# Expert weights: each load waits for the load three places ahead of it, in place of two

## The chip, the cores and the metric

One core of a Trainium2 chip runs the whole program as one launch. The metric is the device time of a run in microseconds (us); of the kernel before, three runs stand below, and one further execution was recorded by the hardware profiler. All rows in this document come from that one recorded execution unless something else is said.

## The reference, cut to what matters

Two transformer blocks run one after the other on 512 tokens of 1024 features in float32. The first block (dilated attention, a gated recurrence, an MLP) and the first half of the second (gated linear attention, a state-space layer) end in a router, and what follows it is a mixture of experts with 32 experts, of which each token takes 4:

```python
def moe_ffn(h, router_w, router_b, w_gu, b_gu, w_down, b_down):
    logits = (xt @ router_w + router_b).astype(f32)
    top_val, top_idx = lax.top_k(logits, TOP_K)          # 4 of 32
    gate = jax.nn.softmax(top_val, axis=-1)
    ...
    def expert_block(args):
        xblk, e = args
        gu = xblk @ w_gu[e] + b_gu[e]                    # 1024 -> 2048
        g, up = gu[:, :D_FF_2], gu[:, D_FF_2:]
        g = jnp.minimum(g, SWIGLU_LIMIT)
        up = jnp.clip(up, -SWIGLU_LIMIT, SWIGLU_LIMIT)
        act = (up + 1.0) * (g * jax.nn.sigmoid(SWIGLU_ALPHA * g))
        return act @ w_down[e] + b_down[e]               # 1024 -> 1024
    ...
    out = zeros.at[tok_buf].add(yb * w_buf[:, None])
```

The weights of one expert are 8 MB for `w_gu` and 4 MB for `w_down`; all 32 experts together are 384 MB, read once from HBM.

## The kernel before

The blocks ahead of the experts take roughly the first 980 us. They aren't touched. Everything around the change is in the class `Moe` (from line 1329).

**Weights.** `order` (L1760) fixes the sequence of the loads: the eight `gu` loads of expert 0, then for each expert e the eight `gu` loads of expert e+1 and the four `dn` loads of expert e. That is 32 x 12 = 384 loads of 1 MB each. `load` (L1625) takes the next of them, gives it the next of 21 slots in SBUF in turn (`RING = 5, 16`), and issues it on SyncE's queue: L1635 for a `gu` load (tile `wgu`, 128 rows of 8 KB) and L1638 for a `dn` load (tile `wdn`). A load into a slot waits until TensorE has read the slot's former weights for the last time. Besides that, `turn` (L1642) makes each load wait for the landing of an earlier one:

```python
        if limit and len(self.flight) >= FLIGHT:
            self.g.tc.add_manual_dep(d, self.flight[-FLIGHT], ... DependencyClass.Sync ..., reason="few loads at a time")
        self.flight.append(d.name)
```

`flight` lists all loads in the order of issue, so with `FLIGHT = 2` at most two are under way. The first five loads are issued before the router is through, with `limit` False, that is without this wait; the other 16 of the first round follow when their slots exist (`buffers`, L1507). SyncE works in order: a load that waits holds back all loads behind it. In the stage of the experts SyncE issues nothing else, apart from reading the experts' token counts and following the branches. `finish` (L1836) sends five small loads through `turn` as well, at the very end.

**Experts.** `run` (L1800) goes through the experts: `tile_up(e)` multiplies the tokens of expert e with the `gu` weights, `tile_down(e-1)` those of the expert before with the `dn` weights, and the loads for the slots that come free are issued behind each (eight, then four). The first 64 tokens of an expert are always computed (L1587 for `gu`, L1617 for `dn`): eight matmuls, two column halves in turn, for each load. Further matmuls run only when the expert has more than 64, 96 or 128 tokens (L1591, and again L1587 and L1617 with the tile `turned`), behind branches on the counts; the expert's weights stay in their slots until these are through. GpSimd gathers the tokens (L1531, `xg`, `x`, `late`), adds the results into HBM (L1623, `acc`), and moves activations of large experts out and in (`spill`, `late`), all on its own DMA queue. TensorE transposes tokens and activations (L1539, `ptx`), VectorE and ScalarE compute the activation (L1560 to L1564) and ScalarE scales the result (L1621).

Of the kernel before, what the change touches and what calls it, by code (L numbers as in the profile page):

```python
# [1316 lines left out]
NCH = T // CH  # L1317
QUARTERS = 2
RING = 5, 16
FLIGHT = 2  # L1320
LATE = 9
PACE = 2
FILLS = 8
# [3 lines left out]
class Moe:  # L1327
# [314 lines left out]
    def turn(self, d, limit=True):  # L1642

        if limit and len(self.flight) >= FLIGHT:
            self.g.tc.add_manual_dep(d, self.flight[-FLIGHT], mybir.DependencyInfo(mybir.DependencyClass.Sync, mybir.DependencyReason.SCHED_ONLY), reason="few loads at a time")
        self.flight.append(d.name)
# [301 lines left out]
```

## Time and profile before

| | us |
|---|---|
| median of 3 runs | 2337.91 |
| lowest, highest | 2332.89, 2342.59 |
| the profiled execution | 2348.3 |
| its span, first to last instruction | 2346.5 |
| TensorE busy in it | 2046.9 |
| stage of the experts, first matmul with expert weights to the last | about 984 to 2310 |

PE is TensorE's matmuls, PEld its weight loads, DVE VectorE, ACT ScalarE, POOL GpSimd, SP SyncE; a q behind an engine's name is its sequencer. The profiled execution was 10.4 us longer than the median of the runs (0.4%). The 16 DMA engines are shown together: their share is the time that packets took, summed over the 16 and divided by 16 times the stretch. The granted clock of TensorE is given as a share of its upper level, 2.4 GHz; 0.961 is the mean of the span.

### The profile page before, as it was taken

How to read it: one execution, taken by the hardware profiler on the slowest of the kernel's cores; microseconds unless marked ns; L12 is line 12 of the kernel's file. 1: busy time of each engine (PE TensorE's matmuls, PEld its weight loads, DVE VectorE, ACT ScalarE, POOL GpSimd, SP SyncE). 2: the span in 40 equal slices, each digit the busy share in tenths (PEclk: the TensorE clock that was granted, in tenths of full speed). 3: DMA queues.
4: the chain of work that ended last, by engine and by line, in shares of the span. 5: the costliest groups of instructions: out<-in, count | busy, mean ns of one | idle time of the engine just before them, and what ended most of it. 6: DMA issues, size and time to landing. Idle time of an engine off the chain costs nothing. (4 is left out here: it accounts for less than half of the span.)

```text
span 2346.5 us, 31249 instructions
## 1 busy us (share of the span) xinstructions
PE 2046.9 (87%) x11586; PEld 1116.4 (48%) x11589; DVE 860.5 (37%) x1891; ACT 476.4 (20%) x839; POOL 333.1 (14%) x329
## 2 busy tenths in 40 slices
PE   6999988999998999789898997766798899898763
PEld 6856765688877977533333332221233333333211
DVE  6466659764556556522121121111121122121112
ACT  3345332234434124200100100000000110000001
POOL 2000226310013221100101101000001110101002
PEclk9999999999999999789999999999999999999997
DMA  6451476852237625898939899999996799999986
GB/s 194 119 169 52 154 195 187 252 175 92 98 104 213 213 75 196 345 337 292 327 143 323 300 337 331 356 329 337 325 356 231 257 329 330 336 349 342 333 323 204
DMA packets 213970, 584.24 MB, mean 249 GB/s; under 512 B 32287, under 2 KB 107438, under 8 KB 179822
## 3 DMA queue, kind: packets, MB, share of 16 engines
q1 hardware_dynamic: 182688, 523.74, 62.3%
q0 software_dynamic: 16784, 46.94, 7.4%
q10 hardware_dynamic: 14142, 9.10, 1.3%
q8 instruction: 189, 3.10, 0.5%
q14 instruction: 167, 1.37, 0.2%
HBM read 537.88 MB, written 41.84 MB: 247 GB/s over the span
## 5 line engine op out<-in xcount | busy, mean ns | idle before, releaser
L1587 PE MATMUL pg<-wgu,xT 128*64 128x512 f32 x1024 | 281.5, 620 | 77.9 <-DMA wgu<-in_exp_w_gu 72.5
L1587 PE MATMUL pu<-wgu,xT 128*64 128x512 f32 x1024 | 272.5, 603 | 3.5 <-issue 3.5
L1617 PE MATMUL py<-wdn,aT 128*64 128x512 f32 x1024 | 241.7, 604 | 34.0 <-DMA wdn<-in_exp_w_down 33.9
L1547 DVE TENSOR_TENSOR turned<-ptx,cols 128x512 f32<-128x512 f32 x42 | 29.1, 692 | 461.7 <-PE ptx L1539 460.4
L1561 ACT ACTIVATE th<-gm 128x512 f32<-128x512 f32 (+1 forms) x54 | 30.2, 560 | 777.4 <-DVE gm L1560 762.9
L89 DVE TENSOR_TENSOR wlo<-wst,whi 128x1024 fp32r<-128x1024 f32 (+1 forms) x109 | 135.4, 1242 | 126.6 <-ACT whi L88 126.5
L88 ACT CAST whi<-wst 128x1024 fp32r<-128x1024 f32 (+2 forms) x121 | 123.9, 1027 | 257.7 <-DMA wst<-in_w_ff_in 82.5
L1587 PEld LDWEIGHTS pg<-wgu,xT 128*64 128x64 f32 x1024 | 66.7, 139 | 228.5 <-DMA wgu<-in_exp_w_gu 124.5
L1587 PEld LDWEIGHTS pu<-wgu,xT 128*64 128x64 f32 x1024 | 76.6, 140 | 155.1 <-issue 155.1
L1623 POOL DMA_INDIRECT acc<-y,idx x54 | 85.7, 1587 | 445.5 <-ACTq L1745 226.0
L1617 PEld LDWEIGHTS py<-wdn,aT 128*64 128x64 f32 x1024 | 66.2, 136 | 166.4 <-issue 105.8
L1657 DVE CAST sel<-pick 128x128 fp32r<-128x128 f32 x32 | 7.7, 239 | 357.5 <-PEq L1735 151.1
L1591 PE MATMUL pgu<-wgu,turned 128*32 128x512 f32 x1152 | 128.6, 594 | 0.0
L98 PE MATMUL pf<-hTh,whi 128*128 128x512 f32 (+1 forms) x288 | 111.2, 390 | 8.6 <-ACT whi L88 6.2
L100 PE MATMUL pf<-hTh,wlo 128*128 128x512 f32 (+1 forms) x288 | 109.5, 383 | 6.9 <-DVE wlo L89 6.9
L99 PE MATMUL pf<-hTl,whi 128*128 128x512 f32 (+1 forms) x288 | 109.5, 381 | 0.0
L1531 POOL DMA_INDIRECT xg<-hn,idx x32 | 33.1, 1033 | 491.8 <-PE ptx L1539 415.5
L1617 PE MATMUL py<-wdn,turned 128*32 128x256 f32 (+1 forms) x1280 | 101.2, 418 | 0.0
L98 PE MATMUL plt<-whi,ahi 128*128 128x512 f32 x256 | 99.6, 389 | 0.0
L99 PE MATMUL plt<-wlo,ahi 128*128 128x512 f32 x256 | 99.6, 389 | 0.0
L100 PE MATMUL plt<-whi,alo 128*128 128x512 f32 x256 | 99.1, 389 | 0.0
L1560 DVE TENSOR_SCALAR gm<-pg 128x512 f32<-128x512 f32 x36 | 24.9, 691 | 155.0 <-PE pg L1587 150.4
(541 smaller groups left out, 3423.8 us busy)
## 6 DMA issues: line engine op xcount, KB each, us to landing
wgu<-in_exp_w_gu SPq DMA_DIRECT2D x256, 1024.0 KB
wdn<-in_exp_w_down SPq DMA_DIRECT2D x128, 1024.0 KB
wst<-in_w_in SPq DMA_DIRECT2D x36, 512.0 KB
wst<-in_w_ff_in SPq DMA_DIRECT2D x32, 512.0 KB
wst<-in_w_ff_out SPq DMA_DIRECT2D x32, 512.0 KB
ada_w<-in_ada_w SPq DMA_DIRECT2D x24, 512.0 KB
a<-in_ada_w SPq DMA_DIRECT2D x24, 512.0 KB
wst<-in_w_out SPq DMA_DIRECT2D x16, 512.0 KB
```

The lines of the kernel that those rows point to most:

```text
L88: g.nc.scalar.copy(hi, st)
L89: eng.tensor_tensor(out=lo, in0=st, in1=hi.bitcast(F32), op=ALU.subtract)
L98: g.nc.tensor.matmul(out, ah, bh, start=start, stop=False)
L99: g.nc.tensor.matmul(out, ah, bl, start=False, stop=False)
L100: g.nc.tensor.matmul(out, al, bh, start=False, stop=stop)
L1531: self.g.nc.gpsimd.indirect_dma_start(out=x, out_offset=None, in_=self.hn, in_offset=bass.IndirectOffsetOnAxis(ap=self.idx[2][:, c, e:e + ...
L1547: g.nc.vector.tensor_tensor(out=out, in0=src, in1=col(1), op=ALU.mult)
L1561: nc.scalar.activation(th, gm, AF.Tanh, scale=0.851)
L1587: nc.tensor.matmul(ps[h * w:(h + 1) * w, :], lhs, W[k][:, o + h * N:o + (h + 1) * N], start=False, stop=(k == KD - 1))
L1591: nc.tensor.matmul(both[h * w:(h + 1) * w], lhs, wk[:, h], start=False, stop=(k == KD - 1))
L1617: nc.tensor.matmul(py[h * w:(h + 1) * w, :], lhs, W[k // 2][:, o:o + N], start=False, stop=(k == KD - 1))
L1623: nc.gpsimd.indirect_dma_start(out=acc, out_offset=bass.IndirectOffsetOnAxis(ap=self.idx[n][:, c, e:e + 1], axis=0), in_=y, in_offset=None ...
```

## The change

```diff
--- before.py
+++ after.py
@@ -1317,7 +1317,7 @@
 NCH = T // CH
 QUARTERS = 2
 RING = 5, 16
-FLIGHT = 2
+FLIGHT = 3
 LATE = 9
 PACE = 2
 FILLS = 8
```

`FLIGHT` is read in `turn` alone. A load that went through `turn` with `limit` now waits for the landing of the load three places ahead of it in `flight`, and no longer for that two places ahead. The order of the loads, the slots, the waits for slots and all other instructions are written as before.

## Rows read from the trace of the kernel before

**Rows 1.** The page, 40 slices of 58.7 us: TensorE's busy tenths, GB/s of all DMAs
```profile
PE   6999988999998999789898997766798899898763
GB/s 194 119 169 52 154 195 187 252 175 92 98 104 213 213 75 196 345 337 292 327 143 323 300 337 331 356 329 337 325 356 231 257 329 330 336 349 342 333 323 204
```

**Rows 2.** Busy time by stretch: stretch, length, five engines (instructions), TensorE clock, DMA share, GB/s
```profile
984.00:1323.00 339.00, 310.37 (x1858) 111.84 (x1858) 63.23 (x113) 26.77 (x47) 38.95 (x32) 0.95 0.80 288
1410.00:1686.00 276.00, 192.49 (x892) 59.79 (x896) 40.51 (x69) 18.07 (x29) 22.69 (x18) 0.98 0.93 336
1880.00:2157.00 277.00, 261.88 (x1658) 96.38 (x1654) 56.56 (x104) 26.02 (x45) 33.57 (x25) 0.99 0.94 340
2157.00:2278.00 121.00, 83.19 (x351) 24.41 (x351) 17.60 (x30) 7.54 (x12) 7.81 (x6) 0.97 0.92 331
```

**Rows 3.** TensorE's waits from 1410 to 1686: who, for what, us, times, longest
```profile
PE pg L1587 <- DMA wgu<-in_exp_w_gu: 46.5, 35, 4.7
PE py L1617 <- DMA wdn<-in_exp_w_down: 24.5, 20, 2.3
```

**Rows 4.** TensorE's waits from 2157 to 2278
```profile
PE pg L1587 <- DMA wgu<-in_exp_w_gu: 26.0, 22, 3.7
PE py L1617 <- DMA wdn<-in_exp_w_down: 9.5, 8, 1.9
```

**Rows 5.** Timeline of TensorE: start, us, what, count [idle before it and what ended it]
```profile
1567.62 1.94 PE L1617 MATMUL py<-wdn,aT 128*64 128x512 f32 x8 [1.36 <-DMA wdn<-in_exp_w_down]
...
2298.91 7.09 PE L1617 MATMUL py<-wdn,aT 128*64 128x512 f32 x32
```

**Rows 6.** SyncE's waits from 1323 to 1686: who, for what, us, times, longest
```profile
SPq L1635 <- DMA wgu<-in_exp_w_gu: 154.9, 54, 6.2
SPq L1638 <- DMA wdn<-in_exp_w_down: 53.8, 17, 5.3
SPq L1635 <- DMA wdn<-in_exp_w_down: 50.6, 18, 3.9
SPq L1638 <- DMA wgu<-in_exp_w_gu: 49.2, 18, 4.4
SPq L1638 <- PEq L1713: 5.0, 1, 5.0
```

**Rows 7.** Load issues from 1323 to 1686, by line: count, ns min/median/max, first and last start
```profile
L1635 SPq DMA_DIRECT2D wgu<-in_exp_w_gu x72: 327/328/341, 1332.9 to 1674.3; - x72
...
L1638 SPq DMA_DIRECT2D wdn<-in_exp_w_down x37: 367/378/920, 1323.1 to 1680.4; - x37
```

**Rows 8.** Load issues from 1880 to 2278, by line
```profile
L1635 SPq DMA_DIRECT2D wgu<-in_exp_w_gu x80: 327/328/341, 1890.0 to 2270.3; - x80
...
L1638 SPq DMA_DIRECT2D wdn<-in_exp_w_down x41: 367/378/422, 1880.3 to 2277.4; - x41
```

**Rows 9.** Load issues of L1635 from 945 to 951, then from 914 to 918
```profile
L1635 SPq DMA_DIRECT2D wgu<-in_exp_w_gu x3: 328/328/383, 945.7 to 950.4; - x3
...
L1635 SPq DMA_DIRECT2D wgu<-in_exp_w_gu x5: 328/422/685, 914.5 to 917.6; - x5
```

**Rows 10.** Busy time from 921 to 929, columns as in rows 2
```profile
921.00:929.00 8.00, 8.00 (x49) 6.38 (x49) 3.82 (x11) 2.27 (x7) 0.00 (x0) 1.00 0.99 415
```

**Rows 11.** DMA queues from 1410 to 1686: packets, MB, share of 16 engines
```profile
q1 hardware_dynamic: 15458, 87.24, 85.4%
q0 software_dynamic: 2032, 4.85, 6.8%
q8 instruction: 27, 0.44, 0.6%
```

**Rows 12.** All DMA issues, GpSimd's indirect ones: count, median us from issue to landing
```profile
acc<-y,idx POOLq DMA_INDIRECT x54, 7.6
xg<-hn,idx POOLq DMA_INDIRECT x32, 6.3
```

**Rows 13.** TensorE's waits from 1686 to 2157, the longest alone
```profile
PE ptx L1539 <- DMA late<-spill: 7.5, 1, 7.5
```

## The prediction

> **What bounds the kernel now.** I read the slices of the page first. TensorE is busy for 9 tenths or so of most slices, but there are two dips, around slices 24 to 27 and at the end, and in both the DMAs move 323 to 356 GB/s [rows 1]. So I cut the stage of the experts into stretches. In those from 984 to 1323 and from 1880 to 2157 TensorE is busy for 310 of 339 and 262 of 277 us; from 1410 to 1686 (A) it is busy for 192.5 of 276 and from 2157 to 2278 (B) for 83.2 of 121 [rows 2]. The view of TensorE's waits names what is missing in A and B: weights. In A it waits 46.5 + 24.5 = 71.0 us in 55 pieces for loads [rows 3], in B 26.0 + 9.5 = 35.5 us in 30 pieces [rows 4]; from 984 to 1323 and from 1686 to 2157 that view has no such line.
>
> These rows are a little short. Eight matmuls on one load are shown as 1.94 us when they stand alone, but 32 in a row as 7.09 [rows 5]: the other 24 took 7.09 - 1.94 = 5.15 us, or 1.72 for each eight, so the last matmul's modelled end hides 0.22 us of each wait. With it A has 71.0 + 55 x 0.22 = 83 us and B 35.5 + 30 x 0.22 = 42 us of real waiting. Their sum, 125 us, is what endless bandwidth could give and no more.
>
> Then the queue of the loads. From 1323 to 1686 SyncE waits 154.9 + 53.8 + 50.6 + 49.2 = 308.5 us for landings, in 107 pieces, and 5 us for a slot [rows 6], while it issues 72 + 37 = 109 loads between 1323.1 and 1680.4 [rows 7]: 357.3 / 108 = 3.31 us a load. From 1880 to 2278 it is 121 loads from 1880.3 to 2277.4 [rows 8], again 397.1 / 120 = 3.31. So the stage alternates: TensorE sets the pace while experts with many tokens pass, the loads set it in A and B, and there the wait in `turn` is what ends last before nearly every issue.
>
> **What the change moves.** It removes nothing and adds nothing but the choice of which landing a load waits for; a third load may be under way. Why could that be faster, when the DMA engines show 0.93 busy in A [rows 2]? Two rows say that the 3.31 us are not the engines' own pace. First, a load alone takes long: of three issues from 945.7 to 950.4 the third waits for the landing of the first [rows 9], so a single load needs about 4.7 us, of which the transfer is only a part. Second, the first five loads were issued without the wait, within 3.1 us [rows 9], and while they were streaming the engines moved 415 GB/s at a share of 0.99 [rows 10]. A load of 1.0486 MB then takes 2.53 us, or 2.50 at a full share. In A the loads' queue moved 87.24 MB in a share of 0.854 of 276 us [rows 11], which is 316 GB/s, or 370 for a full share: packets are 419 / 370 = 1.13 times as long as in that undisturbed stretch. My reading is that with two loads in flight the engines that finish early run dry until the slowest has landed and the next load has been issued and started, and that the first packets after such a pause carry the latency. A third load covers a pause of one whole load.
>
> **The price of a load afterwards.** Gathers, scatters and instruction fetches keep their share of the engines, 6.8% + 0.6% and a little [rows 11], say 7.5%. If the rest went to weights at the undisturbed pace, a load would take 2.50 / 0.925 = 2.70 us. That is one end. The other end: packets stay as long as they are in A and only the idle 7% goes; the loads then get 0.925 of 370 GB/s, 342 GB/s, and a load takes 3.06 us. No row of the kernel shows three in flight. I take the near end, since the stream of five is the same kind of load without the wait, and leave 2% for engines that still run dry: 2.70 / 0.98 = 2.76 us. Each load saves 3.31 - 2.76 = 0.55 us.
>
> **Where that reaches the end.**
> - From 984 to 1323: nothing is gained directly, since TensorE never waits for weights there; SyncE will be stopped by slots more often, which costs nothing.
> - A: the loads are the bound without a break from 1323 on. 109 x 0.55 = 60 us. The stretch has 83 us of waiting, so all 60 count, and some 23 us of waiting are left.
> - B: its own 37 loads give 37 x 0.55 = 20 us. On top comes a reserve: from 1880 to 2157 TensorE sets the pace, and the 84 loads there can run ahead by up to 46 us, as far as the 21 slots let them. Together they would cover all 42 us of waiting. The slots won't be full, because an expert with more than 64 tokens keeps its weights until its last chunk; of the reserve I count 16 us and take 36, with 20 and 42 as ends.
> - The beginning (fills) and the end: TensorE starts on the experts some 65 us after the first five loads were issued, and after the last weights the end is scatters and the final norm. Nothing there.
>
> The sum is 60 + 36 = 96 us. The profiled execution of 2348.3 us would become 2252; it was 10.4 us above the median of the runs, and I carry that over, 2337.9 - 96 = 2242 us. At 2.70 us a load it would be 66 + 38 = 104 (2234); at 3.06, 27 + 22 = 49 (2289). The floor is all waiting gone, 2338 - 125 = 2213.
>
> **What is queued behind the wait.** Behind a waiting load on SyncE stand only further loads and its branches, so an earlier release delays nobody there. GpSimd's gathers and scatters use the same 16 engines, and that is the place where harm could come from (third rival).
>
> **The rivals.**
> 1. *A ceiling of the memory.* The best slices of the whole stage show 356 GB/s [rows 1], and if that is what HBM gives under steady load, about 20 GB/s for the others (4.85 + 0.44 MB and a little in 276 us [rows 11]) leave 336 for weights: 3.12 us a load. A then gains 109 x 0.19 = 21, B some 17, and the time is 2300. For it: 356 appears twice and never more. Against it: the 415 GB/s of the stream of five [rows 10], though over 8 us only. Chance 0.2. The Trainium skill speaks for this rival: DMA: Bandwidth & Descriptors, Specifications, gives a limit of about 358 GB/s of HBM for one core, far under the 435 GB/s of its fabric. The row of 415 GB/s disagrees with it as long as eight microseconds count.
> 2. *One engine is the slow one.* If the same one of the 16 engines is always late, it is busy without a break already, and a third load only waits longer behind it. The shares are means of 16 engines and can't exclude one at 1.0. Then nothing changes: 2338. Against it: the stream of five ran at 0.99, where a steady straggler would have let the others idle. Chance 0.1. That the wait isn't the one that ends last, and the change so does nothing, has the same time; the 5 us of waiting for slots beside 308 for landings [rows 6] leave it 0.02.
> 3. *Slower, by late gathers.* A gather lands 6.3 us after its issue and a scatter 7.6 [rows 12]; a third load in the same engines may push each by its own transfer, about 2.5 us. With 54 scatters and 32 gathers of `xg`, 86 x 2.5 = 215 us would be added to GpSimd's chain. Now TensorE waits for such a DMA rarely, the longest 7.5 us, once in 470 us [rows 13]. The kernel gets slower than before only if more than 96 / 2.5 = 38 of the 86 are exposed. Time if half are: 2242 + 108 = 2350. Chance 0.05, because most gathers are issued an expert ahead. The same page of the Trainium skill, Queues, rings and completion order, says that an engine takes turns between its queues packet by packet; by that rule a gather would not stand behind the whole third load. No row here shows it.
>
> **How the numbers follow.** The forecast (a load at 2.65 to 2.95 us) has 0.63, the ceiling 0.2, no change 0.12, slower 0.05. The predicted time is 2242. The range goes from the floor of 2213 to 2300, which takes in both ends of the load's price and the ceiling and leaves out 0.17. About 0.5% (12 us) is what a measurement of this kernel can tell from no change. The forecast and the ceiling are faster by more than that, 0.83; no change is 0.12; slower 0.05.
>
> **What would show it.** Right: from 1323 on issues 2.7 to 2.9 us apart in the DMA-bound stretches, a share of 0.96 or more and 380 GB/s or more there; TensorE's waits for `wgu` and `wdn` down from 106 us to 20 to 40; more of SyncE's waiting on slots; the rows of GpSimd's landings up by less than 2 us. The ceiling would show as a share near 1.0 at 356 GB/s, with longer packets. The slow engine would show as the same 3.31 us with longer time from issue to landing. The prediction is wrong if a load takes more than 3.1 us, or if TensorE's waits go from weights to gathered tokens (`ptx`) by tens of microseconds.

## The result, and the profile after

The kernel after takes 2262.18 us (median of 3 runs, 2259.86 to 2262.80), against 2337.91 before: a ratio of 0.966 with a 95% interval of 0.963 to 0.970, or 75.7 us less. The profiled execution took 2262.18 us, which is 86.1 less than the profiled one of before (2348.3). 2242 had been forecast, in a range from 2213 to 2300.

The page after, the two lines that answer to [rows 1]: TensorE's busy tenths, and GB/s of all DMAs in slices of 56.5 us.

```profile
PE   6999988999998999978899799987898899999993
GB/s 193 109 199 38 129 224 155 238 219 113 98 94 188 189 166 67 296 353 311 395 295 117 308 301 403 398 401 391 408 386 182 254 306 363 384 288 398 401 397 185
```

The two dips in TensorE's line are gone. No slice of before moved more than 356 GB/s; here twelve do, and eleven of them stand at 384 to 408. The same by stretch, columns as in [rows 2]; 1410 to 1621 is what A has become (the same experts), 2080 to 2187 what B has become, with about one expert more:

```profile
1324.00:1410.00 86.00, 80.69 (x411) 28.25 (x411) 18.92 (x34) 7.88 (x13) 8.91 (x7) 1.00 1.01 393
1410.00:1621.00 211.00, 179.98 (x841) 62.20 (x841) 39.23 (x68) 18.05 (x29) 20.80 (x16) 0.95 1.02 399
1842.00:2080.00 238.00, 221.77 (x1461) 81.45 (x1462) 45.77 (x84) 21.27 (x38) 29.35 (x22) 0.98 0.93 360
2080.00:2187.00 107.00, 101.20 (x479) 35.77 (x476) 23.35 (x40) 10.05 (x16) 10.37 (x8) 1.00 1.02 398
```

A share of 1.02 means that the recorded times of packets overlap a little; it is to be read as full. The queues in A, answering to [rows 11]: packets, MB, share of 16 engines.

```profile
q1 hardware_dynamic: 13967, 79.34, 93.0%
...
```

The loads now move 79.34 MB in 211 us at a share of 0.93, 376 GB/s, or 404 for a full share; before it was 370. So the packets have become shorter, though not quite as short as in the stream of five (419). The issues from 1324 to 1621, answering to [rows 7]:

```profile
L1635 SPq DMA_DIRECT2D wgu<-in_exp_w_gu x72: 327/328/341, 1329.5 to 1618.1; - x72
...
L1638 SPq DMA_DIRECT2D wdn<-in_exp_w_down x36: 367/378/907, 1324.1 to 1620.6; - x36
```

These are 108 loads from 1324.1 to 1620.6: 296.5 / 107 = 2.77 us a load, where 3.31 stood and 2.76 was forecast. TensorE's waits in A, answering to [rows 3] (who, for what, us, times, longest):

```profile
PE ptx L1539 <- PEq L1745: 16.9, 6, 4.6
PE py L1617 <- DMA wdn<-in_exp_w_down: 5.5, 9, 1.4
...
PE pg L1587 <- DMA wgu<-in_exp_w_gu: 1.4, 2, 1.0
```

Of 71.0 us of waiting for weights 6.9 are left there. But another wait now leads the list: the transposes at L1539 that follow the branch of L1745. That is the branch behind an expert's first 64 tokens in `tile_down`, and PEq is TensorE's own sequencer, not another engine. Over the whole span, first before, then after:

```profile
PE ptx L1539 <- DMA late<-spill: 14.2, 2, 7.5
PE ptx L1539 <- PEq L1745: 13.5, 20, 2.5
...
PE ptx L1539 <- PEq L1735: 10.1, 6, 3.6
```

```profile
PE ptx L1539 <- PEq L1745: 32.5, 20, 4.6
...
PE ptx L1539 <- DMA late<-spill: 19.1, 2, 10.3
PE ptx L1539 <- PEq L1735: 14.2, 6, 5.2
...
PE py L1617 <- DMA wdn<-in_exp_w_down: 5.5, 9, 1.4
...
PE pg L1587 <- DMA wgu<-in_exp_w_gu: 2.3, 4, 1.0
```

The waits for weights fell from 106.4 us to 7.8. The three other waits shown (behind L1745, behind L1735, for spilled activations) rose from 37.8 us to 65.8, by 28.0. One of these waits in the timeline of TensorE (start, us, what, count, idle before it), and then the busy time during the wait, just behind it and later (columns as in [rows 2]):

```profile
1543.75 1.11 PE L1539 MATMUL ptx<-ident,act 128*128 128x128 f32 x4 [4.56 <-PEq L1745]
```

```profile
1541.00:1543.60 2.60, 0.00 (x0) 0.00 (x0) 0.10 (x1) 0.00 (x0) 0.82 (x1) 1.00 1.02 400
1543.70:1547.00 3.30, 3.25 (x10) 1.78 (x12) 0.12 (x2) 0.60 (x1) 0.00 (x0) 0.50 1.05 338
1547.10:1551.00 3.90, 3.90 (x20) 1.26 (x18) 0.00 (x0) 0.00 (x0) 0.00 (x0) 1.00 1.01 393
```

TensorE stands for 4.56 us at the branch, and then the granted clock is 0.50 (1.2 GHz) for 3.3 us before it is 1.00 again. While it stood, the DMA engines moved 400 GB/s. So some of the waiting for weights has turned into waiting for something else. Over the whole stage of the experts (984 to 2299 before, 981 to 2215 after, the same 6430 matmuls) the clock is 0.97 in both kernels.

### The profile page after: what moved, and what is told of

It is laid out like the page before. It is cut to its first block, busy times and chain, and to the rows that moved or that the text cites. A ratio compares the mean times of both kernels' runs of the same rounds, so it can differ in the third digit from the quotient of the medians.

```text
span 2260.5 us, 31247 instructions
## 1 busy us (share of the span) xinstructions
PE 2032.5 (90%) x11586; PEld 1121.9 (50%) x11589; DVE 855.9 (38%) x1891; ACT 476.3 (21%) x839; POOL 331.6 (15%) x329
## 5 line engine op out<-in xcount | busy, mean ns | idle before, releaser
L1617 PE MATMUL py<-wdn,aT 128*64 128x512 f32 x1024 | 236.3, 599 | 5.5 <-DMA wdn<-in_exp_w_down 5.5
L1539 PE MATMUL ptx<-ident,act 128*128 128x128 f32 x256 | 44.1, 298 | 59.7 <-PEq L1745 32.5
```

Source lines behind the costliest of these rows:

```text
L1539: d = g.nc.tensor.transpose(pt[:, b * P:(b + 1) * P], x[:, b * P:(b + 1) * P], g.ident)
L1617: nc.tensor.matmul(py[h * w:(h + 1) * w, :], lhs, W[k // 2][:, o:o + N], start=False, stop=(k == KD - 1))
```

## The experiments

Two questions were open. Is it the time between issue and landing that had set the price of a load, and is three the end of it? And why does TensorE wait longer at branches and for spilled activations now?

**Four loads and eight.** `FLIGHT = 4` and `FLIGHT = 8` in place of 3.

> Four loads under way in place of three, nothing else. Theory A (the third load covers the pause between a landing and the next load's first packets; what it does not give back is code for TensorE's branches that arrives a fixed time after its request): the pause is covered already, so loads in the stretches that they bound come 2.65 to 2.8 us apart, TensorE's waits for weights stay at 10 us or fall to 5, its idle time behind the branch of L1745 stays at 30 to 35 us; time 2252 to 2262. Rival B (each further load under way delays the other transfers, code and spilled activations above all): the idle time behind L1745, 13.5 us with two loads and 32.5 with three, goes to 45 or more; time 2270 to 2285.

> Eight loads under way. Theory A: the engines are full with three, so 2.65 to 2.8 us a load, waits for weights 10 us or less and time 2255 to 2268, as with three and four. Rival B (depth delays code, gathers and spills): TensorE's idle time on them grows with each load under way; time 2275 or more.

Measured: 2262.94 us with four (0.965 of before, 0.961 to 0.968) and 2262.32 with eight (0.966, 0.961 to 0.971): the kernel after, within its spread. A load took 2.75 and 2.64 us between the issues of the 102nd and the 209th. The second figure is too low as a price: with eight under way the first seven issues of that stretch only fill the queue. From the 109th issue to the 205th, when it is full in each run, it is 2.78, 2.79 and 2.79 us with three, four and eight. The rows of four, then of eight:

```profile
PE ptx L1539 <- PEq L1745: 30.6, 20, 4.4
...
PE py L1617 <- DMA wdn<-in_exp_w_down: 5.0, 9, 0.9
PE pg L1587 <- DMA wgu<-in_exp_w_gu: 4.0, 6, 1.4
```

```profile
PE ptx L1539 <- PEq L1745: 26.9, 20, 4.8
...
PE pg L1587 <- DMA wgu<-in_exp_w_gu: 7.4, 9, 1.8
```

Three fill the engines. Rival B, that each further load costs the other transfers more, falls: behind L1745 it is 32.5, 30.6 and 26.9 us with three, four and eight, and the median scatter lands 9.2, 9.4 and 9.6 us after its issue (7.6 before). The time with four was just above what theory A had given, within the spread of the runs.

**One load.** `FLIGHT = 1`.

> One load under way at a time. Theory A (the price of a load is the time from its issue to its landing divided by the loads under way, until the engines are full): a lone load took about 4.7 us, so loads come 4.7 to 5.2 us apart; the 363 loads behind the first 21 then set the pace of nearly the whole stage, which ends near 1000 + 363 x 4.95 = 2800; time 2750 to 2900. Rival (the engines' own pace is 3.3 us and the two in flight already fill them): one under way costs little, under 4 us a load, time under 2550.

Measured: 3000.67 us, one execution, above the range of either theory. The issues from 1450 to 2027:

```profile
L1635 SPq DMA_DIRECT2D wgu<-in_exp_w_gu x72: 327/328/341, 1467.2 to 2021.5; - x72
...
L1638 SPq DMA_DIRECT2D wdn<-in_exp_w_down x36: 367/373/379, 1450.4 to 2026.3; - x36
```

108 loads in 575.9 us are 5.38 us a load, a little over what was expected, and with it theory A's own sum gives 1000 + 363 x 5.38 = 2953. The 4.7 us of [rows 9] were taken ahead of the experts, with no gather or scatter under way (and a second load issued 0.4 us behind the first); that this makes the difference is argued, not shown. With one, two, three and four under way a load costs 5.38, 3.31, 2.77 and 2.75 us; times the number under way that is 5.4, 6.6, 8.3 and 11.0 us from issue to landing (worked out, not measured). From one to two this time grows by 23% only, so the price falls steeply; from three to four it grows in proportion, and the price stands still. The rival's price of under 4 us and its 2550 us are far off.

**The same amount in smaller pieces.** Each load of 1 MB is issued as two of 512 KB, and the wait counts halves, with 4, 6 and 8 in turn:

```diff
-            if kind == "gu":
-                d = g.nc.sync.dma_start(w, ...[0, e, k * P:(k + 1) * P, :])
-            ...
-            self.turn(d.ins, limit)
+            for h in range(2):
+                ... src = the h-th half of the columns (gu) or of the rows (dn)
+                self.turn(g.nc.sync.dma_start(w[:, h * D:(h + 1) * D], src).ins, limit, h)
...
-        if limit and len(self.flight) >= FLIGHT:
-            self.g.tc.add_manual_dep(d, self.flight[-FLIGHT], ...)
+        if limit and len(self.halves) >= FLIGHT:
+            self.g.tc.add_manual_dep(d, self.halves[-FLIGHT], ...)
```

> Each load of 1 MB is issued as two of 512 KB, and each of these waits for the landing of the one four places ahead of it: 2 MB under way as in the kernel before, but the next transfer is released while up to 1.5 MB, and not 1 MB, are still queued. Theory A (what counts is how much is still queued when the release comes): the pause is mostly covered, 1 MB takes 2.8 to 3.0 us in the stretches that the loads bound, TensorE's waits for weights fall from 106 us to 15 to 45; time 2262 to 2290. Rival C (what counts is the amount under way at most): 3.3 us for each MB as before, waits for weights near 106 us; time 2330 to 2345.

> Halves of 512 KB again, now six under way: 3 MB, as in the kernel after. Theory A, as the run with four halves leaves it (the amount under way decides, whatever the size of the pieces): 1 MB takes 2.75 to 2.85 us in the stretches that the loads bound, time 2255 to 2275. Rival (each transfer has a cost of its own, and there are twice as many): 3.0 to 3.2 us for 1 MB, time 2300 to 2335.

> Halves of 512 KB, eight under way, 4 MB. Theory A (the amount under way decides until the engines are full): a price of 2.7 to 2.8 us for 1 MB, waits for weights back to 15 us or less; if the code waits stay at the 18.5 us of the run with six halves, 2245 to 2258, if they go back to the 32 us of whole loads, 2258 to 2268. Rival (each transfer costs something, so halves stay dearer): 2.8 us or more and 2268 to 2280.

Measured: 2331.13 us with four halves (0.996, 0.993 to 0.999), 2270.26 with six (0.970, 0.964 to 0.976), 2269.74 with eight (0.972, 0.968 to 0.975). In the stretch that the loads bound, the issues of four halves, then of six:

```profile
L1639 SPq DMA_DIRECT2D wgu<-in_exp_w_gu x144: 327/328/731, 1332.4 to 1662.7; - x144
L1639 SPq DMA_DIRECT2D wdn<-in_exp_w_down x70: 327/328/1368, 1323.0 to 1636.9; - x70
```

```profile
L1639 SPq DMA_DIRECT2D wgu<-in_exp_w_gu x144: 327/328/483, 1329.3 to 1625.5; - x144
L1639 SPq DMA_DIRECT2D wdn<-in_exp_w_down x71: 327/328/994, 1325.4 to 1626.8; - x71
```

1 MB takes 2 x 339.7 / 213 = 3.19 us with four halves and 2 x 301.4 / 214 = 2.82 with six; with eight it is 2.80. The first of the three expectations was wrong: I had held that an earlier release, with 1.5 MB still queued, would cover most of the pause, and 3.19 is much nearer to the 3.31 of two whole loads. The third missed too: 2269.74 us lies in its rival's range (halves stay dearer). Over the same full stretch as above, the 109th to the 205th MB, six halves cost 2.83 and eight 2.84, where whole loads cost 2.78 to 2.79, and waits for weights are 21.6 us with eight halves, where 15 or less had been expected. So the amount under way decides most, 2 MB or 3 MB, and the size of the pieces some 2%. The engines were at a share of 0.98 with four halves and yet moved only 346 GB/s:

```profile
DMA packets 33161, 118.13 MB, mean 346 GB/s; under 512 B 3754, under 2 KB 3882, under 8 KB 33077
...
q1 hardware_dynamic: 30533, 111.21, 89.5%
```

So a share near 1 does not say that the engines are at their pace: the missing time stands in the packets' own durations.

**Half the loads left out.** `order` keeps the loads of even experts, and an odd expert uses its neighbour's weights; `load` is called half as often, and the odd experts' own weights are never read. Once with three under way, once with two.

```diff
-        gu = lambda e: [("gu", e, k) for k in range(KD)]
-        dn = lambda e: [("dn", e, k) for k in range(KD // 2)]
+        gu = lambda e: [("gu", e, k) for k in range(KD)] if e % 2 == 0 else []
+        dn = lambda e: [("dn", e, k) for k in range(KD // 2)] if e % 2 == 0 else []
...
             self.W.setdefault((kind, e), []).append(w)
+            self.W[kind, e + 1] = self.W[kind, e]
```

> Three loads under way, but weights are loaded for even experts only and each odd expert computes with the weights of the expert before it, so half the loads are left out and TensorE should not wait for weights at all. Theory A: code for the branch still comes about 8 us after its hint, while TensorE reaches the branch 5.4 us after it, so the idle time behind L1745 stays at 25 to 40 us although the DMA engines are half idle; time 2240 to 2255. Rival B: with the DMA engines half idle the code is there in time, idle time behind L1745 under 13 us; time 2215 to 2230.

> As the run before (half the loads left out), but two loads under way. Theory A: no wait for weights either, so the same time as with three loads under way within 5 us, and the same idle time behind L1745 within 5 us. Rival B: less delay of the other transfers than with three, idle time behind L1745 lower by 10 us or more, time lower by 10 or more.

Measured: 2190.97 us with three and 2178.39 with two, one execution each; the first is below the ranges of both theories, by 24 us and more. Theory A had said that code comes a fixed time after its request, and so would be late here too. It falls by its sign, the wait behind the branch. TensorE's waits with three under way, and then with two:

```profile
PE ptx L1539 <- PEq L1746: 11.7, 20, 3.9
...
PE ptx L1539 <- DMA late<-spill: 2.8, 2, 2.2
```

```profile
PE ptx L1539 <- PEq L1746: 9.3, 20, 1.2
...
PE ptx L1539 <- DMA late<-spill: 3.3, 2, 2.3
```

(L1746 is L1745 of the kernel after, one line down.) The wait behind the branch goes from 32.5 us to 11.7 and that for spilled activations from 19.1 to 2.8, together 37 us. The branch itself, in the view of that line: count, ns min/median/max; before, after, and with half the loads and three under way:

```profile
L1745 PEldq COMPARE_BRANCH  x32: 68/446/4548, 1028.9 to 2302.0; - x32
```

```profile
L1745 PEldq COMPARE_BRANCH  x32: 68/2586/6297, 1023.7 to 2217.2; - x32
```

```profile
L1746 PEldq COMPARE_BRANCH  x32: 68/458/6851, 1023.3 to 2147.1; - x32
```

The median hides two groups. In every run twelve of the 32 take less than 0.1 us. The other twenty take 2.2 to 6.3 us in the kernel after; with half the loads ten of them take 0.43 to 0.87 us and ten take 2.6 to 6.9. There the stream of loads runs and rests in turn with the experts: in the 3 us ahead of each long one the DMA engines moved 300 GB/s or more, ahead of each short one less than 100. Two neighbours of that run, the branch and then the 3 us ahead of it (columns as in [rows 2]):

```profile
L1746 PEldq COMPARE_BRANCH  x1: 2884/2884/2884, 1540.2 to 1540.2; - x1
L1746 PEldq COMPARE_BRANCH  x1: 478/478/478, 1565.4 to 1565.4; - x1
```

```profile
1537.20:1540.20 3.00, 3.00 (x17) 0.76 (x13) 1.13 (x2) 0.00 (x0) 0.00 (x0) 1.00 1.01 414
1562.40:1565.40 3.00, 3.00 (x16) 0.78 (x12) 1.18 (x2) 0.00 (x0) 0.79 (x1) 1.00 0.03 8
```

In both the hint came 5.5 us ahead of the branch. So the branch takes long while a full stream of loads runs, and depth is not what matters: eight under way are no worse than three. Whether the code waits at the DMA engines or at the memory is not separated. A second reason stands beside it: in A the hint now comes 5.5 to 9.5 us ahead of the branch, where it was 10.3 to 12.6, as TensorE hardly waits for weights in between. It isn't needed for the rise, since eleven of the twenty had about 5.5 us in both kernels and went from 2.2 us in the mean to 3.9. That the run with two was 12.6 us faster than that with three is one execution against one, and the waits shown account for 2 us of it; whether depth costs something where the engines are not full stays open.

**The hint for the branch.** The kernel asks for a branch's code ahead of it, with a hint. In one run the hint for the branch of the down projection is given earlier, in `tile_up` right behind the hint of the up projection; in the other it is left out.

```diff
 def tile_up(self, e, xT):
-        self.up(2, e, xT, act0, mid=lambda: self.transposed(self.x1, self.turned(1)))
+        def mid():
+            self.transposed(self.x1, self.turned(1))
+            if e:
+                self.early = self.hinted(e - 1, CH, "down")
+        self.up(2, e, xT, act0, mid=mid)
```

```diff
 def run(self):
-                more = self.hinted(e - 1, CH, "down")
+                more = None
```

> Three loads under way as in the kernel after; the hint that asks for the code of the branch behind the first 64 tokens' down projection is issued some 15 us earlier, right behind the hint for the branch of the up projection. Theory D (what the change gave back is TensorE waiting for code that is asked for too late when the load stream never pauses): idle time behind that branch falls from 32 us to under 15, time 2235 to 2252. Rival E (a second hint displaces the first, or changes nothing): the waits move to the branch of the up projection or stay; time 2260 to 2300.

> Three loads under way; the hint ahead of the down projection, which asks for the code behind the branch of L1745, is left out. Theory F (with the stream of loads never pausing, code arrives 3 us or more too late, and the hint still hides some of it): without it each of the 20 branches to code that isn't there takes about 6 us in place of 2.6 in the median, idle time behind it rises from 32 us to 60 to 90; time 2285 to 2315. Rival (the hint does nothing under a full stream): 2255 to 2268.

Measured: 2313.99 us with the early hint (0.988 of before, 0.984 to 0.991), 51.8 more than the kernel after and above the range of either theory; 2340.82 without it (1.000, 0.998 to 1.003), 78.6 more. With the early hint, TensorE's waits (L1751 is L1745 of the kernel after, six lines down) and the branch of the up projection (now L1719; in the kernel after it is L1713, with a median of 352 ns):

```profile
PE ptx L1539 <- PEq L1751: 43.3, 20, 4.1
PE ptx L1539 <- PEq L1719: 33.9, 20, 2.6
```

```profile
L1719 PEldq COMPARE_BRANCH  x32: 70/4190/6173, 996.0 to 2249.1; - x32
```

Rival E it is, by its sign: the second hint seems to take the place of the first, for the up projection's branch now takes 3.5 to 6.2 us in nineteen of its twenty longer cases. The early hint itself did its work for eight of the twenty longer branches of the down projection (0.46 us) and not for the other twelve (3.7 to 6.8). So this run doesn't tell whether an earlier request alone would help; it tells that two outstanding at once did not both hold. Without the hint:

```profile
PE ptx L1539 <- PEq L1745: 61.6, 20, 4.1
PE pg L1587 <- issue: 27.4, 11, 3.7
```

```profile
L1745 PEldq COMPARE_BRANCH  x32: 65/5874/7032, 1027.3 to 2297.6; - x32
```

A branch to code that nobody asked for takes 3.6 to 7.0 us (the twenty longer ones), against 2.2 to 6.3 with the hint and a full stream, where eight of the twenty gain little (4.7 us and more). The 61.6 us lie in the expected range; the time lies above it, because waits came up at the start of the next up projection too (27.4 us, the second line), which I had not thought of. The hint is worth some 79 us, and a full stream of loads takes a part of its use away. No run that loads all weights is faster than the kernel after.

## Why the prediction was right in size of the load, and off in the sum

- **What bounds.** Right for A and B. The loads set the pace there, by their landings; with more under way the waits for weights fell from 106.4 us to 7.8. From 1842 to 2080 TensorE is busy for 222 of 238 us, much as in the third line of [rows 2], and there nothing was gained.
- **The price of a load.** 2.76 us forecast, 2.77 measured. That [rows 9] and [rows 10] were taken for more than the engines' share was the step that carried it; the runs with one to eight loads confirm it. That it fits to 0.01 us is luck: the ends stood at 2.70 and 3.06, and the 2% between 2.70 and 2.76 were a guess. One detail is only half of it: the engines do not simply run dry. From before to after the share in A rose from 0.93 to 1.02 and the loads' rate at a full share from 370 to 404 GB/s, so about half of the missing rate was idle time and half sat in long packets; the run with four halves moved 346 GB/s at a share of 0.98.
- **The ceiling of the memory** did not hold. Over 86 and 211 us the engines moved 393 and 399 GB/s, and 403 with eight loads. The figure of about 358 GB/s in the Trainium skill (DMA: Bandwidth & Descriptors, Specifications) does not bind here; the measurement decides. **The one slow engine** falls with the same numbers.
- **A, B and what lies between.** The first matmul of each up projection (L1574) gives the same marks in both kernels: first A, before and after, then the stretch from A to shortly ahead of B.

```profile
L1574 PE MATMUL pg<-bias,sel x11: 467/496/774, 1332.8 to 1698.3; 128*128 128x512 f32 x11
L1574 PE MATMUL pg<-bias,sel x11: 476/502/776, 1333.9 to 1644.3; 128*128 128x512 f32 x11
L1574 PE MATMUL pg<-bias,sel x12: 475/498/776, 1698.3 to 2118.4; 128*128 128x512 f32 x12
L1574 PE MATMUL pg<-bias,sel x12: 475/491/775, 1644.3 to 2071.5; 128*128 128x512 f32 x12
```

  A took 365.5 us and takes 310.4: 55 less, where 60 were forecast. From there to the span's end it is 39 less (228.1 to 189.0), where B's term was 36; that the reserve in it, picked between two ends, came out so near is partly luck. The stretch between takes 427.2 in place of 420.1, 7 more, and ahead of A 1 more is lost; the prediction had nothing there. 55 + 39 - 7 - 1 = 86 us, against 96. So the largest miss is a term put at nothing: the stretch in which TensorE sets the pace got slower.
- **What is next late.** That is the step missing in the sum. I put the new waits into a rival that ended above 2337.9 and gave it 0.05, instead of taking a part of them as a term; code for branches was nowhere in the prediction, although [rows 11] has its queue. Between A and B the wait for spilled activations went from 7.5 us to 10.3 and that behind L1735 from 5.9 to 8.4, which is 5.3 of the 7 us. But the 28.0 us more of such waits are not 28 us lost. In A the wait behind L1745 rose from 5.9 us to 16.9, and yet A is bound by the loads in both kernels: SyncE now stands for landings for 248 of 297 us, and the engines' share is 1.02. What TensorE waits at a branch there, it would otherwise wait for weights. Three, four and eight loads fit that: 32.5, 30.6 and 26.9 us behind L1745, 7.8, 9.0 and 10.5 for weights, and the same time. No run removes the waits at branches alone, so this is argued.
- **The waits as a sum.** With the 0.22 us a piece of the prediction, the waits for weights went from 125 us (85 pieces) to 11 (13 pieces): 114 us gone, where 96 had been counted and 20 to 40 us had been expected to stay. TensorE's other idle time rose by 27 us, its busy time but for that correction by 1, and 114 - 27 - 1 is the 86 of the two profiled executions. The prediction had called itself wrong if waits went to `ptx` for gathered tokens by tens of microseconds; `ptx` did gain such waits, but for branches and spilled activations. The clock is not a term: it fell in A from 0.98 to 0.95, but over the stage it stayed at 0.97.
- **The gathers.** Their landings rose, but not by a whole load's transfer. Median us from issue to landing, answering to [rows 12]:

```profile
acc<-y,idx POOLq DMA_INDIRECT x54, 9.2
xg<-hn,idx POOLq DMA_INDIRECT x32, 7.3
```

  That is 1.6 and 1.0 us more, under the 2 us that the prediction allowed, and of GpSimd's transfers TensorE waits for little but the spilled activations. The Trainium skill's rule of taking turns (DMA: Bandwidth & Descriptors, Queues, rings and completion order) goes with this, and so does the run with eight loads, where five more loads ahead raised the two medians by 0.4 and 0.2 us only.
- **The 10.4 us** by which the profiled execution of before stood above its median were carried over to the kernel after, which has no such offset: its profiled execution is its median. In later sets the runs of before ranged from 2330 to 2355, while the three runs of the kernel after lie within 3 us. Half of the 20 us between 2242 and 2262 is this, the other half is the sum: 5 us in A, 7 between A and B and 1 ahead of A, less 3 in B.

## What to carry to other kernels

A queue that waits for a landing before it issues has a price of its own: the time from issue to landing divided by the transfers under way, until the engines are full. Look for a place in the same kernel where transfers were issued without the wait, and take the price from there, not from the busy share of the engines. When such a wait goes, ask what else the same engines bring, branch code and spilled data above all, and put that into the sum as a term with its own rows, for the stretches in which the transfers do not set the pace.

## What the runs showed of the hardware

- Loads of 1 MB from HBM, alone on their queue: 5.38, 3.31, 2.77 and 2.75 us each with 1, 2, 3 and 4 MB under way, and no less with 8 MB once the queue is full (2.79); pieces of 512 KB with 2, 3 and 4 MB under way: 3.19, 2.82 and 2.80 us for 1 MB.
- The engines' share can be 0.98 at 346 GB/s and 1.02 at 399 GB/s.
- One branch of TensorE, in the twenty executions of 32 that took over 0.1 us: 3.6 to 7.0 us without a hint, 2.2 to 6.3 with the hint beside a full stream of loads; in the run with half the loads 2.6 to 6.9 us behind 3 us in which the DMA engines moved 300 GB/s or more, and 0.43 to 0.87 behind 3 us with less than 100. A second hint behind the first made the first one's branch take 4.2 us in the median in place of 0.35.
- Scatters of GpSimd landed 7.6, 9.2, 9.4 and 9.6 us (median) after their issue with 2, 3, 4 and 8 MB of loads under way.
- After a wait of 4.56 us the granted clock was 0.50 for 3.3 us.
